# Operand halves moved from GpSimd to VectorE, and pooling and Fourier steps reordered, in an fp32 hybrid encoder layer

## Chip, cores and metric

One core of a Trainium2 chip runs the whole kernel. The metric is the device time of one execution in microseconds; the time given for a kernel is the median over its runs.

## What is computed

One encoder layer over two sequences, 4096 and 2048 tokens of 1024 channels, all in float32:

```python
h = rms_norm(x, pre_g)
proj = jnp.einsum('bsd,de->bse', h, w_in)
a_u, a_v, a_gate, b_in, b_gate, c_in, c_gate = jnp.split(proj, offsets, axis=-1)
ya = mixer_a(a_u, a_v, a_ln_g, a_ln_b, a_w_s, a_b_s) * jax.nn.silu(a_gate)  # gMLP, 128x128 mix per head
yb = mixer_b(b_in, b_w, b_scale) * jax.nn.silu(b_gate)   # centred means over 2, 4, 8, 16 tokens, minus identity
yc = mixer_c(c_in, c_w) * jax.nn.silu(c_gate)            # real part of a 2-D Fourier transform, per 64 channels
y = jnp.einsum('bse,ed->bsd', jnp.concatenate([ya, yb, yc], axis=-1), w_out)
return x + rms_norm(y, post_g)
```

## The kernel before

Every large matrix product is done in the seven-product form of fast matrix multiplication: operands and weights are cut into quadrants, summed, and multiplied seven times; the products are named P1, P2, X1, X2, Y1, X3 and Y2. Each factor is a float32 number in two parts: ScalarE rounds it to a high part (`split`, L137, a CAST in the trace) and a subtraction gives the low part (L138, TENSOR_TENSOR). TensorE then multiplies high by high, low by high and high by low (`mm3`, L141 to L143). The low part of an operand is 128x2048 and is made as two halves of 128x1024; before the change VectorE makes one half and GpSimd the other.

There are four passes. The first (0 to 490 us) goes over 12 blocks of 512 tokens: it normalises, makes the seven operands of a block (`operands`, four sums L177 to L191), stores them in DRAM and multiplies them for the Fourier branch. A scheduler orders its instructions. The second (490 to 959 us, operands b_P1 and so on) loads the operands again for the pooling branch, and the third (959 to 1437 us, a_P1 and so on) does so for the gMLP branch. The fourth, from 1437 us, is the output projection with its own operands.

The second and third pass are written by hand as slots, six blocks of 1024 tokens with seven slots each, one slot for each product. A slot loads the operand of two slots later, cuts the operand of the next slot (cast and low halves), and runs three products, one for each of three channel tiles (PSUM tiles Pb, Ab and Yb in the second pass, Pa, Ya and Aa in the third). Between them stand `fill_a` and `fill_b` (pooling, gating, normalising), the evictions of PSUM by `evict`, and `beside`, which runs one step of the Fourier branch. Four engines and the DMA queue of SyncE (SP) all execute in the order written. The slot of X1 adds to the PSUM banks that P1 has just filled, after the copy of P1's product (zb, L1318) has been made on ScalarE.

`beside` is called twice in a slot. A step has up to four parts: `load`, `pre`, `compute` and `store`. `steps` is a list: tables of the gMLP and channel mix (`table_steps`; their matmul prs reads ws), ten folds (`fold_steps`; VectorE subtractions L949 and L951, then a split), and the transforms (levels, `eg` and `T`; base steps; mix steps, whose matmuls pmx read the split th and tl, and at the end of each pair pny, which reads cny). `normalise` (L1408) issues 16 activations on ScalarE; it stands in `fill_a` of the third pass's slots P2 and X3.

Of the kernel before, what the change touches and what calls it, by code (L numbers as in the profile page):

```python
# [33 lines left out]
def hybrid_encoder(  # L34
# [722 lines left out]
    for b in range(NB):  # L757
        blk = nblk
        if b + 1 < NB:
            nxs = load_x(b + 1, xt, "p")  # L760
            nblk = Block(b + 1)
        for i, m in enumerate(ORDER):
            op = ready.pop(0)
            if b > 0 or i > 2:
                blk.product(m, op)
            if b == 0 and 0 < i < 4:
                rest_of_weights(i)
            if b > 0 or i > 1:
# [116 lines left out]
    def table_steps():  # L885
# [211 lines left out]
    def mix_steps(s, pair, kb):  # L1097
# [49 lines left out]
        if kb == S // 2 // TB - 1:  # L1147
            out[1] = Step(compute_ny, load_ny, None, store_ny)
# [63 lines left out]
    def pool_means(z, n, t, name, corr_at=None):  # L1212
# [7 lines left out]
        if t == 0:  # L1220
            V.tensor_add(b[96:, to], a[96:, 7 : n + 7], a[96:, 9 : n + 9])
            nc.scalar.copy(a[96:, to], b[96:, to])
        else:
            V.tensor_add(b[:, 2 : n + 15], a[:, 1 : n + 14], a[:, 3 : n + 16])
            if t == 1:
                V.tensor_add(a[64:, to], b[64:, 6 : n + 6], b[64:, 10 : n + 10])
                nc.scalar.copy(a[0:64, to], b[0:64, to])
            else:
                c = e1.tile([P, TB + 16], F32, tag="w", name=f"pc{name}", bufs=2)
                V.tensor_add(c[:, 4 : n + 13], b[:, 2 : n + 11], b[:, 6 : n + 15])  # L1230
                V.tensor_add(a[0:96, to], c[0:96, 4 : n + 4], c[0:96, 12 : n + 12])
                nc.scalar.copy(a[96:, to], c[96:, to])
# [4 lines left out]
        return a  # L1237

    class PoolBlock:


        def __init__(self, b):
# [59 lines left out]
        def close_sequence(self):  # L1302
# [30 lines left out]
    for b in range(NB // 2):  # L1333
        blk = PoolBlock(b)
        pairs = [Wide(t, f"b{b}_{t}") for t in range(3)]
        p = before
        means = lambda who, h, t: lambda: who.means(h, t)
        fa = {
            0: [lambda: blk.new_z(0)], 1: [lambda: blk.new_g(0)], 2: [],
            3: [lambda: blk.new_g(1), means(blk, 0, 0)], 4: [means(blk, 0, 2)],  # L1340
            5: [lambda: blk.new_z(1), lambda: blk.silu(1)], 6: [blk.keep_ends, means(blk, 1, 0)],
        }
        fb = {i: [] for i in range(7)}
        fb[3], fb[6] = [means(blk, 0, 1)], [means(blk, 1, 1)]
        if p:
            fa[0] += [lambda: p.silu(0), lambda: p.means(1, 2)]
            fb[0] += [lambda: p.gate(0)]
            fa[1] += [lambda: p.gate(1)]
            fa[2] += [p.close_sequence]
        for i, m in enumerate(WIDE["b"]):  # L1350
# [7 lines left out]
            slot(7 * b + i, pairs, lambda t, ps, m=m, blk=blk: blk.evict(m, t, ps), fa[i], fb[i], loads, None, cuts)  # L1358
        before = blk
# [194 lines left out]
    for b in range(NB // 2):  # L1554
# [38 lines left out]
        for i, m in enumerate(WIDE["a"]):  # L1593
            ev = lambda t, ps, m=m, blk=blk: blk.evict(m, t, ps)
            j = 7 * (b + NB // 2) + i
            if b == 0 and i == 0:
# [283 lines left out]
```

## Time and profile before

| | us |
|---|---|
| median of 3 runs | 1918.48 (1915.41 to 1920.11) |
| the profiled execution | 1926.82 |
| its span | 1925.0 |
| TensorE busy | 1762.3 (92% of the span) |
| VectorE busy | 1384.2 (72%) |
| ScalarE busy | 919.4 (48%) |
| GpSimd busy | 839.7 (44%) |

Busy time of an engine counts from start to end of each instruction, with whatever it waits inside. The granted TensorE clock was 0.96 of full speed on the mean.

### The profile page before, as it was taken

The numbers are of one execution on the slowest core, as the hardware profiler recorded it, in microseconds if no ns is written. First come the engines' busy times: TensorE is split into PE (matmuls) and PEld (weight loads), VectorE is DVE, ScalarE is ACT, GpSimd is POOL, SyncE is SP. The second block draws the span as 40 slices with busy tenths as digits, with TensorE's granted clock in tenths as the row PEclk, the third lists the DMA queues.
The fourth block names the chain that finished last, engine by engine and source line by source line (L and its number), as shares of the span: only waits on it lengthen the run. The fifth ranks groups of instructions, "written<-read, shape, count | busy, mean of one in ns | idle before, by whom it ended". The sixth has DMA issues, their size and how long they took to land. (4 is left out here: it accounts for less than half of the span.)

```text
span 1925.0 us, 27890 instructions
## 1 busy us (share of the span) xinstructions
PE 1762.3 (92%) x9784; PEld 1509.0 (78%) x9784; DVE 1384.2 (72%) x2163; ACT 919.4 (48%) x1766; POOL 839.7 (44%) x464
## 2 busy tenths in 40 slices
PE   5999999999878887988879999899988999999998
PEld 5999999999767666877668778787766888888876
DVE  8877767777588787667666575555677777877776
ACT  4766654444454443435445554555663433333332
POOL 6433664675332222222332332223355666666664
PEclk9999999999999998999889999999998999999999
DMA  6999997896669877757676675765644454545443
GB/s 243 316 335 313 368 343 271 290 325 234 224 217 307 263 253 252 260 202 236 232 258 228 234 256 188 246 206 195 198 156 159 159 169 158 170 159 169 158 160 109
DMA packets 221787, 443.84 MB, mean 231 GB/s; under 512 B 30416, under 2 KB 112976, under 8 KB 221648
## 3 DMA queue, kind: packets, MB, share of 16 engines
q1 hardware_dynamic: 221648, 442.07, 67.1%
q8 instruction: 77, 1.26, 0.3%
q14 instruction: 62, 0.51, 0.1%
HBM read 297.81 MB, written 150.47 MB: 233 GB/s over the span
## 5 line engine op out<-in xcount | busy, mean ns | idle before, releaser
L1712 POOL TENSOR_TENSOR cc<-cc,xr 128x1024 f32<-128x1024 f32 x46 | 110.3, 2398 | 53.5 <-DVE cc L1711 53.5
L1408 ACT ACTIVATE vn<-vn,lnst 128x96 f32<-128x96 f32 x192 | 70.2, 453 | 54.6 <-DVE lnst L1403 54.6
L398 DVE SCALAR_TENSOR_TENSOR xp<-xp,g_sb,rbc 128x256 f32<-128x256 f32 x192 | 92.5, 549 | 2.1 <-PE rbc L607 1.3
L1653 ACT ACTIVATE junk<-cc 128x512 f32<-128x512 f32 x72 | 45.5, 632 | 86.3 <-DVE cc L1694 51.8
L137 ACT CAST yo_X<-y 128x512 fp32r<-128x512 f32 x60 | 34.9, 620 | 87.9 <-PE Xo L143 71.9
L138 DVE TENSOR_TENSOR yo_P<-y,yo_P 128x512 fp32r<-128x512 f32 x48 | 69.5, 1449 | 6.4 <-ACT yo_P L137 6.1
L1711 DVE SCALAR_TENSOR_TENSOR cc<-cc,orr,pgb 128x512 f32<-128x512 f32 x69 | 53.8, 807 | 15.2 <-POOL orr L1661 15.2
L1218 DVE TENSOR_TENSOR pa<-zb 128x527 f32<-128x527 f32 x36 | 64.5, 1792 | 0.0
L1661 POOL TENSOR_TENSOR orr<-oms,mhalf 128x1 f32<-128x1 f32 x48 | 27.0, 562 | 84.5 <-DVE oms L1659 84.5
L177 POOL TENSOR_TENSOR s<-xp,xp 128x1024 f32<-128x1024 f32 x11 | 26.5, 2408 | 82.5 <-DVE xp L398 68.5
L138 DVE TENSOR_TENSOR yo_X<-y,yo_X 128x512 fp32r<-128x512 f32 x48 | 58.9, 1227 | 0.2
L365 ACT ACTIVATE xrow<-xrow 128x512 f32<-128x512 f32 x88 | 54.8, 627 | 7.3 <-DMA xrow<-in_x_sample 7.2
L141 PE MATMUL Ab<-b_X1h,wbX1h 128*128 128x512 f32 x72 | 32.6, 453 | 21.1 <-ACT zb L1318 21.1
L177 DVE TENSOR_TENSOR ys<-y,y 128x512 f32<-128x512 f32 x24 | 27.1, 1132 | 34.2 <-DMA y<-yc_d 33.8
L1653 ACT ACTIVATE junk<-Po 128x512 f32<-128x512 f32 x24 | 14.4, 599 | 74.7 <-PE Po L143 74.7
L1398 POOL TENSOR_TENSOR lnst<-lnst,mhalf 128x16 f32<-128x16 f32 x12 | 35.7, 2972 | 29.2 <-DVE lnst L1397 29.2
L137 ACT CAST yo_P<-y 128x512 fp32r<-128x512 f32 x48 | 29.4, 614 | 39.1 <-PE Xo L143 26.1
L191 POOL TENSOR_TENSOR y<-y,y 128x512 f32<-128x512 f32 x23 | 31.5, 1369 | 35.0 <-DVE yo_X L138 29.4
L1394 DVE BATCH_NORM_STATS2 lnst<-vn 128x6 f32<-128x96 f32 x192 | 44.1, 230 | 0.0
L138 POOL TENSOR_TENSOR a_X3l<-a_X3l,a_X3h 128x1024 fp32r<-128x1024 f32 x6 | 14.6, 2438 | 64.8 <-ACT a_X3h L137 64.8
L138 POOL TENSOR_TENSOR a_Y2l<-a_Y2l,a_Y2h 128x1024 fp32r<-128x1024 f32 x6 | 14.5, 2422 | 63.8 <-ACT a_Y2h L137 50.1
L377 DVE TENSOR_SCALAR diag<-ident,rr 128x128 f32<-128x128 f32 x44 | 40.9, 982 | 1.9 <-POOL rr L353 1.1
(778 smaller groups left out, 7122.7 us busy)
## 6 DMA issues: line engine op xcount, KB each, us to landing
op_d<-xp SPq DMA_DIRECT2D x72, 512.0 KB, 5.0
mt<-const_m SPq DMA_DIRECT2D x56, 512.0 KB, 6.4
xp<-in_xt SPq DMA_DIRECT2D x48, 512.0 KB, 5.5
out<-cc SPq DMA_DIRECT2D x46, 512.0 KB, 2.9
xr<-in_x_sample SPq DMA_DIRECT2D x32, 512.0 KB, 4.3
xrow<-in_x_sample SPq DMA_DIRECT2D x28, 512.0 KB, 5.7
o<-o_d SPq DMA_DIRECT2D x40, 256.0 KB, 5.7
vn_d<-vg SPq DMA_DIRECT2D x48, 192.0 KB, 3.6
```

The lines of the kernel that those rows point to most:

```text
L137: last_cast[0] = nc.scalar.copy(hi, src)
L138: return (nc.gpsimd if pool_lo else nc.vector).tensor_sub(lo, src, hi.bitcast(F32))
L177: e[0].tensor_add(s1, a21, a22)
L365: nc.scalar.activation(half, half, AF.Square, accum_out=ss[:, 2 * c + h : 2 * c + h + 1])
L377: nc.vector.tensor_scalar_mul(diag[:, c], ident, rr[:, 2 * a + c : 2 * a + c + 1])
L398: nc.vector.scalar_tensor_tensor(xs[q][:, sl], xs[q][:, sl], g8_sb[:, 4 * kh + k : 4 * kh + k + 1], rbc[a], ALU.mult, ALU.mult,)
L1218: V.tensor_add(a[:, 1 : n + 16], z[:, 0 : n + 15], z[:, 1 : n + 16])
L1394: nc.vector.bn_stats(st[:, j], self.v[h][c][:, 96 * hd : 96 * hd + 96])
L1408: nc.scalar.activation(v_, v_, AF.Identity, bias=nb[:, j : j + 1], scale=rv[:, j : j + 1])
L1653: nc.scalar.activation(junk, src, AF.Square, accum_out=ss[:, j : j + 1])
L1711: nc.vector.scalar_tensor_tensor(cc[c][:, hs], src, rr, pgb[:, hs], ALU.mult, ALU.mult)
L1712: nc.gpsimd.tensor_add(cc[c], cc[c], xr[c])
```

## The change

1. In the first pass all operand sums and the low parts of X2 and X3, which GpSimd made, go to VectorE; in the second and third pass VectorE makes both halves of each low part, and the low parts of the wide weights and of the output weights.
2. `pool_means` becomes a generator with a stop between its sums with the ScalarE copy and its last step on VectorE (`sums`, then `means` one place later); in a P1 slot the sums stand ahead of the three silu activations.
3. A step's `pre` runs two steps ahead of its `compute` instead of one, its `store` two behind instead of one; the four table steps move behind two folds and become six, and each base pair gets one empty step behind it.
4. In a second-pass slot the stores of yb go behind the first eviction, three at a time. The tiles of gny and cny get a ring of their own, and cny is made in a `pre`. One `next_y` is issued earlier at the start of the fourth pass.

```diff
-    SUMS0 = (nc.gpsimd, nc.vector, nc.gpsimd, nc.gpsimd)
+    SUMS0 = (nc.vector,) * 4
...
-    make = make_operand("p0", ("X2", "X3"))
+    make = make_operand("p0")
...
-                split(lo[:, h].bitcast(F32), hi[:, h], lo[:, h], h == 1)
+                split(lo[:, h].bitcast(F32), hi[:, h], lo[:, h])
...
-        for eng, sl in ((nc.vector, slice(0, 2)), (nc.gpsimd, slice(2, 3))):
-            eng.tensor_sub(lo[:, sl], lo[:, sl].bitcast(F32), hi[:, sl].bitcast(F32))
+        nc.vector.tensor_sub(lo, lo.bitcast(F32), hi.bitcast(F32))
...
-        if i <= len(steps):
-            part(i - 1, "store")
+        if i <= len(steps) + 1:
+            part(i - 2, "store")
             part(i + 2, "load")
             part(i, "compute")
-            part(i + 1, "pre")
+            part(i + 2, "pre")
...
-        return [Step(compute, load), Step(compute_mix, load_mix), Step(), Step()]
+        return [Step(), Step(), Step(compute, load), Step(compute_mix, load_mix), Step(), Step()]
...
-        return [Step(load), copies.pop(0), Step(compute), Step(store)]
+        return [Step(load), copies.pop(0), Step(compute, store=store), Step()]
...
         for which in range(2):
             out.append(base_step(s, pair, which))
+        out.append(Step())
...
+        def prepare_ny():
+            st["c"] = fpool.tile([P, 1], F32, tag="n", name=f"cny{nm}", bufs=4)
+            nc.scalar.activation(st["c"], T_of[(s, pair)][:, S // 2 : S // 2 + 1], AF.Copy, scale=scale)
+
         def compute_ny():
-            col_ = ftile(f"cny{nm}", (P, 1))
-            nc.scalar.activation(col_, T_of[(s, pair)][:, S // 2 : S // 2 + 1], AF.Copy, scale=scale)
...
-    steps[0:0] = table_steps()
+    steps[8:8] = table_steps()
...
-        flush(stores)
+        if not late:
+            flush(stores)
...
         evict(0, ps)
+        if late:
+            done, stores[:] = stores[:late], stores[late:]
+            flush(done)
         beside()
...
-            5: [lambda: blk.new_z(1), lambda: blk.silu(1)], 6: [blk.keep_ends, means(blk, 1, 0)],
+            5: [lambda: blk.new_z(1), lambda: blk.silu(1)], 6: [blk.keep_ends, sums(blk, 1, 0)],
         }
         fb = {i: [] for i in range(7)}
-        fb[3], fb[6] = [means(blk, 0, 1)], [means(blk, 1, 1)]
+        fb[3], fb[6] = ([sums(blk, h, 1), means(blk, h, 0)] for h in range(2))
+        fb[4] = [means(blk, 0, 2)]
         if p:
-            fa[0] += [lambda: p.silu(0), lambda: p.means(1, 2)]
-            fb[0] += [lambda: p.gate(0)]
+            fa[0] += [lambda: p.sums(1, 2), lambda: p.means(1, 1), lambda: p.silu(0)]
+            fb[0] += [lambda: p.means(1, 2), lambda: p.gate(0)]
...
-        split(lo[k].bitcast(F32), hi[k], lo[k], k % 2 == 1)
+        split(lo[k].bitcast(F32), hi[k], lo[k])
...
         cut_out_weights(m)
+        if m == "Y1":
+            next_y()
```

ScalarE at the P1 slot of the second pass's third block, before: the cast of the next operand (X1), the silu of the block before (gb), the last pooling copy (pa from pc), the copy of P1's first product (zb from Ab).

```order
L137 CAST b_X1h<-b_X1l 128x1024 x2
L1261 COPY zb_0_0_6757<-edge 128x16
L1261 COPY zb_0_1_6759<-edge 128x16
L1261 COPY zb_0_2_6761<-edge 128x16
L1274 ACTIVATE gb_0_0_6286<-gb_0_0_6286 128x512
L1276 COPY gb_1_0_6434<-gb_0_0_6286 128x8
L1274 ACTIVATE gb_0_1_6287<-gb_0_1_6287 128x512
L1276 COPY gb_1_1_6435<-gb_0_1_6287 128x8
L1274 ACTIVATE gb_0_2_6288<-gb_0_2_6288 128x512
L1276 COPY gb_1_2_6436<-gb_0_2_6288 128x8
L1232 COPY pa_1_2_6769<-pc_1_2_6773 32x512
L1318 COPY zb_0_0_6757<-Ab_0_6744 128x512
```

The same place on ScalarE in the changed kernel:

```order
L137 CAST b_X1h<-b_X1l 128x1024 x2
L1270 COPY zb_0_0_6728<-edge 128x16
L1270 COPY zb_0_1_6730<-edge 128x16
L1270 COPY zb_0_2_6732<-edge 128x16
L1239 COPY pa_1_2_6734<-pc_1_2_6738 32x512
L1283 ACTIVATE gb_0_0_6265<-gb_0_0_6265 128x512
L1285 COPY gb_1_0_6406<-gb_0_0_6265 128x8
L1283 ACTIVATE gb_0_1_6266<-gb_0_1_6266 128x512
L1285 COPY gb_1_1_6407<-gb_0_1_6266 128x8
L1283 ACTIVATE gb_0_2_6267<-gb_0_2_6267 128x512
L1285 COPY gb_1_2_6408<-gb_0_2_6267 128x8
L1331 COPY zb_0_0_6728<-Ab_0_6715 128x512
```

The pooling copy, which waits for VectorE, now stands ahead of the three silu activations, so these stand between it and the copy of P1's product.

VectorE at the same hand-over, before, from the low half of P1 to the low half of X1 (pa, pb: pooling sums; gb from Yb: eviction of Y2):

```order
L138 TENSOR_TENSOR b_P1l<-b_P1l,b_P1h 128x1024
L1218 TENSOR_TENSOR pa_1_0_6685<-zb_1_0_6595 128x527
L1221 TENSOR_TENSOR pb_1_0_6686<-pa_1_0_6685 32x512
L1236 SCALAR_TENSOR_TENSOR pa_1_0_6685<-pa_1_0_6685,cols,zb_1_0_6595 128x512
L1330 TENSOR_TENSOR gb_0_0_6286<-Yb_0_6513,gb_0_0_6286 128x512
L1218 TENSOR_TENSOR pa_1_1_6712<-zb_1_1_6597 128x527
L1224 TENSOR_TENSOR pb_1_1_6713<-pa_1_1_6712 128x525
L1226 TENSOR_TENSOR pa_1_1_6712<-pb_1_1_6713 64x512
L1236 SCALAR_TENSOR_TENSOR pa_1_1_6712<-pa_1_1_6712,cols,zb_1_1_6597 128x512
L1330 TENSOR_TENSOR gb_0_1_6287<-Yb_1_6544,gb_0_1_6287 128x512
L1330 TENSOR_TENSOR gb_0_2_6288<-Yb_2_6561,gb_0_2_6288 128x512
L138 TENSOR_TENSOR b_X1l<-b_X1l,b_X1h 128x1024
```

The end of the same stretch on VectorE in the changed kernel; the eight subtractions that begin this fold (L948) stand right ahead of these rows, and the two halves of P1 ahead of them:

```order
L950 TENSOR_TENSOR fz_2048_000_6590<-fz_2048_000_6590,fz_2048_004_6592 128x512
L138 TENSOR_TENSOR fo_2048_00_6656<-fo_2048_00_6656,fh_2048_00_6667 128x512
L950 TENSOR_TENSOR fz_2048_012_6594<-fz_2048_012_6594,fz_2048_016_6596 128x512
L138 TENSOR_TENSOR fo_2048_01_6657<-fo_2048_01_6657,fh_2048_01_6671 128x512
L1224 TENSOR_TENSOR pa_1_1_6686<-zb_1_1_6569 128x527
L1230 TENSOR_TENSOR pb_1_1_6687<-pa_1_1_6686 128x525
L1232 TENSOR_TENSOR pa_1_1_6686<-pb_1_1_6687 64x512
L1244 SCALAR_TENSOR_TENSOR pa_1_0_6650<-pa_1_0_6650,cols,zb_1_0_6567 128x512
L1343 TENSOR_TENSOR gb_0_1_6266<-Yb_1_6518,gb_0_1_6266 128x512
L1343 TENSOR_TENSOR gb_0_2_6267<-Yb_2_6533,gb_0_2_6267 128x512
L138 TENSOR_TENSOR b_X1l<-b_X1l,b_X1h 128x1024 x2
L1224 TENSOR_TENSOR pa_1_2_6734<-zb_1_2_6571 128x527
```

Both halves of P1 and X1 are here now, and the last step of each pooling tile (L1236, now L1244) has moved behind the sums of the next.

ScalarE in the P2 slot of the third pass's second block, before (vn: `normalise`):

```order
L137 CAST a_X2h<-a_X2l 128x1024 x2
L1408 ACTIVATE vn_0_9600<-vn_0_9600,lnst_0_9851 128x96 x4
L1408 ACTIVATE vn_1_9602<-vn_1_9602,lnst_0_9851 128x96 x4
L1408 ACTIVATE vn_2_9604<-vn_2_9604,lnst_0_9851 128x96 x4
L1408 ACTIVATE vn_3_9606<-vn_3_9606,lnst_0_9851 128x96 x4
L137 CAST a_X3h<-a_X3l 128x1024 x2
```

and in the changed kernel:

```order
L137 CAST a_X2h<-a_X2l 128x1024 x2
L1423 ACTIVATE vn_0_9567<-vn_0_9567,lnst_0_9822 128x96 x4
L1423 ACTIVATE vn_1_9569<-vn_1_9569,lnst_0_9822 128x96 x4
L1423 ACTIVATE vn_2_9571<-vn_2_9571,lnst_0_9822 128x96 x4
L1423 ACTIVATE vn_3_9573<-vn_3_9573,lnst_0_9822 128x96 x4
L1044 COPY ev_4096_1_9987<-pd_4096_10_9173 128x512
L1045 ACTIVATE eg_4096_1_9988<-pd_4096_10_9173,cols 128x512
L137 CAST a_X3h<-a_X3l 128x1024 x2
```

The work of a level (ev, eg), which stood in the slot before, has come to stand behind the sixteen activations; cny, which stood there in the third, fourth and fifth block, has left these slots.

## Rows read from the trace of the kernel before

**Rows 1.** Windows of the first two passes: length, busy us of each engine, clock, DMA.

```profile
core 0: us, PE busy (x) PEld busy (x) DVE busy (x) ACT busy (x) POOL busy (x), PEclk, DMA share, GB/s
0.00:490.00 490.00, 455.32 (x3202) 448.94 (x3203) 373.56 (x562) 266.15 (x519) 262.60 (x136) 0.98 0.86 303
490.00:959.00 469.00, 399.62 (x1650) 320.96 (x1649) 340.85 (x457) 209.36 (x372) 130.84 (x66) 0.92 0.73 244
```

**Rows 2.** TensorE's waits, 490 to 1437 us: total, times, longest.

```profile
PE Ab L141 <- ACT zb L1318: 21.1, 5, 8.7
PE pny L1140 <- ACT cny L1138: 17.4, 4, 4.5
...
PE pmx L141 <- ACT th L137: 8.8, 3, 4.2
PE prs L901 <- DMA ws<-in_ws_t: 7.2, 1, 7.2
PE pd L141 <- ACT eg L1045: 7.1, 4, 4.4
PE pd L141 <- DMA mt<-const_m: 6.7, 2, 4.6
PE Yb L142 <- DVE b_Y2l L138: 6.5, 2, 3.4
PE Ab L142 <- POOL b_X3l L138: 4.9, 3, 2.0
```

**Rows 3.** Windows of single slots and of pairs of slots, columns as in rows 1.

```profile
591.40:599.56 8.16, 8.16 (x38) 6.76 (x36) 2.98 (x4) 2.48 (x3) 2.43 (x1) 1.00 0.95 272
497.78:515.20 17.42, 10.22 (x46) 7.83 (x44) 7.01 (x11) 5.89 (x9) 3.74 (x5) 0.80 0.60 198
539.68:567.30 27.62, 19.78 (x74) 15.27 (x72) 24.06 (x38) 12.51 (x25) 9.65 (x4) 0.88 0.59 200
567.30:591.40 24.10, 19.26 (x74) 15.34 (x72) 23.69 (x35) 12.67 (x27) 5.85 (x2) 0.86 0.77 269
635.00:660.01 25.01, 19.16 (x74) 15.02 (x72) 22.46 (x35) 12.40 (x26) 8.03 (x3) 0.86 0.73 231
711.16:738.70 27.54, 18.82 (x74) 15.07 (x73) 26.37 (x44) 11.94 (x25) 5.85 (x2) 0.81 0.60 203
...
915.37:931.97 16.60, 12.88 (x44) 9.72 (x43) 12.09 (x14) 5.72 (x7) 4.75 (x2) 0.79 0.51 175
1143.41:1160.01 16.60, 12.31 (x45) 9.72 (x44) 6.13 (x7) 8.41 (x20) 2.43 (x1) 0.79 0.66 221
```

**Rows 4.** Timeline around the P1 slot at 635 us: start, us, engine, instruction.

```profile
632.95 2.90 DVE L1218 TENSOR_TENSOR pa<-zb 128x527 f32<-128x527 f32 x1
...
638.52 0.70 DVE L1218 TENSOR_TENSOR pa<-zb 128x527 f32<-128x527 f32 x1
...
643.79 2.86 DVE L1218 TENSOR_TENSOR pa<-zb 128x527 f32<-128x527 f32 x1
...
642.65 3.43 POOL L138 TENSOR_TENSOR b_X1l<-b_X1l,b_X1h 128x1024 fp32r<-128x1024 f32 x1 [7.37 <-ACT b_X1h L137]
...
642.74 0.63 ACT L1274 ACTIVATE gb<-gb 128x512 f32<-128x512 f32 x1
...
648.16 0.61 ACT L1232 COPY pa<-pc 32x512 f32<-32x512 f32 x1 [3.04 <-DVE pc L1230]
```

**Rows 5.** Window behind the wait that ended at 649.43, columns as in rows 1.

```profile
649.43:656.23 6.80, 6.80 (x20) 5.41 (x21) 6.77 (x17) 4.77 (x10) 0.54 (x1) 0.64 0.38 116
```

**Rows 6.** Groups of instructions: VectorE's half of operand X3, third pass.

```profile
L138 DVE TENSOR_TENSOR a_X3l<-a_X3l,a_X3h 128x1024 fp32r<-128x1024 f32 x6 | 7.4, 1226 | 7.6 <-ACT a_X3h L137 7.6
```

**Rows 7.** Groups of instructions: the activations of `normalise`.

```profile
L1408 ACT ACTIVATE vn<-vn,lnst 128x96 f32<-128x96 f32 x192 | 70.2, 453 | 54.6 <-DVE lnst L1403 54.6
```

**Rows 8.** Windows of a block late in the first pass, and around the fourth pass's start.

```profile
375.20:414.30 39.10, 36.13 (x258) 35.30 (x257) 30.02 (x45) 16.03 (x26) 26.91 (x14) 1.00 0.95 319
...
1424.00:1470.00 46.00, 32.82 (x110) 24.34 (x111) 38.10 (x44) 20.73 (x38) 20.45 (x13) 0.81 0.42 141
```

More of the change, by code (lines that the diff above doesn't have):

```diff
@@ L776, in hybrid_encoder @@
                     stream = operands(
-                        nxs, rpool.tile([P, 1024], F32, tag="s3", name=f"s3_{b + 1}"), make_operand(f"p{b + 1}", ("X2", "X3")),
+                        nxs, rpool.tile([P, 1024], F32, tag="s3", name=f"s3_{b + 1}"), make_operand(f"p{b + 1}"),
                         ORDER, SUMS0, normaliser(b + 1, nxs, nrbc), keep_operand(b + 1),
@@ L1132, in load_ny @@
         def load_ny():
-            st["g"] = ftile(f"gny{nm}", (P, 1))
+            st["g"] = fpool.tile([P, 1], F32, tag="n", name=f"gny{nm}", bufs=4)
             nc.sync.dma_start(st["g"], gc_d[s][rows, S // 2 : S // 2 + 1])
+        def prepare_ny():
+            st["c"] = fpool.tile([P, 1], F32, tag="n", name=f"cny{nm}", bufs=4)
+            nc.scalar.activation(st["c"], T_of[(s, pair)][:, S // 2 : S // 2 + 1], AF.Copy, scale=scale)
         def compute_ny():
-            col_ = ftile(f"cny{nm}", (P, 1))
-            nc.scalar.activation(col_, T_of[(s, pair)][:, S // 2 : S // 2 + 1], AF.Copy, scale=scale)
             ps = wide_bank("G", f"pny{nm}")
-            nc.tensor.matmul(ps[:, 0:1], cmix[pair][0], col_, start=True, stop=True)
+            nc.tensor.matmul(ps[:, 0:1], cmix[pair][0], st["c"], start=True, stop=True)
             nc.vector.tensor_mul(st["g"], st["g"], ps[:, 0:1])
@@ L1147, in mix_steps @@
         if kb == S // 2 // TB - 1:
-            out[1] = Step(compute_ny, load_ny, None, store_ny)
+            out[1] = Step(compute_ny, load_ny, prepare_ny, store_ny)
         return out
@@ L1166, in flush, with slot @@
             f()
-    def slot(j, pairs, evict, fill_a=(), fill_b=(), loads=(), then=None, cuts=()):
+    def slot(j, pairs, evict, fill_a=(), fill_b=(), loads=(), then=None, cuts=(), late=False):
         m = todo[j][2]
         load_operand(j + 2)
-        flush(stores)
+        if not late:
+            flush(stores)
         for f in loads:
@@ L1221, in pool_means @@
             V.tensor_add(b[96:, to], a[96:, 7 : n + 7], a[96:, 9 : n + 9])
-            nc.scalar.copy(a[96:, to], b[96:, to])
+            rows, src = slice(96, P), b
         else:
@@ L1226, in pool_means @@
                 V.tensor_add(a[64:, to], b[64:, 6 : n + 6], b[64:, 10 : n + 10])
-                nc.scalar.copy(a[0:64, to], b[0:64, to])
+                rows, src = slice(0, 64), b
             else:
@@ L1231, in pool_means @@
                 V.tensor_add(a[0:96, to], c[0:96, 4 : n + 4], c[0:96, 12 : n + 12])
-                nc.scalar.copy(a[96:, to], c[96:, to])
+                rows, src = slice(96, P), c
+        nc.scalar.copy(a[rows, to], src[rows, to])
+        yield a
         if corr_at is not None:
@@ L1236, in pool_means @@
         V.scalar_tensor_tensor(a[:, to], a[:, to], invw[t], z[:, to], ALU.mult, ALU.subtract)
-        return a
+        yield a
     class PoolBlock:
@@ L1247, in __init__ @@
             self.pooled = [[None] * 3 for _ in range(2)]
+            self.half = {}
         def new(self, lst, h, tag, extra, bufs):
@@ L1278, in silu, with sums, means @@
                     nc.scalar.copy(ends[t][:, 16:24], self.g[1][t][:, TB : TB + 8])
-        def means(self, h, t):
-            self.pooled[h][t] = pool_means(
+        def sums(self, h, t):
+            self.half[h, t] = pool_means(
                 self.z[h][t], TB, t, f"{self.b}_{h}_{t}", (16, 0) if self.t0 == 0 and h == 0 else None
             )
+            next(self.half[h, t])
+        def means(self, h, t):
+            self.pooled[h][t] = next(self.half[h, t])
         def keep_ends(self):
@@ L1308, in close_sequence @@
                 nc.gpsimd.tensor_copy(zl[t][:, 0:16], ends[t][:, 0:16])
-                a = pool_means(zl[t], 8, t, f"{self.b}_{t}l", (8, 8))
+                *_, a = pool_means(zl[t], 8, t, f"{self.b}_{t}l", (8, 8))
                 nc.vector.tensor_mul(a[:, 8:16], a[:, 8:16], ends[t][:, 16:24])
@@ L1337, in hybrid_encoder @@
         means = lambda who, h, t: lambda: who.means(h, t)
+        sums = lambda who, h, t: lambda: who.sums(h, t)
         fa = {
             0: [lambda: blk.new_z(0)], 1: [lambda: blk.new_g(0)], 2: [],
-            3: [lambda: blk.new_g(1), means(blk, 0, 0)], 4: [means(blk, 0, 2)],
-            5: [lambda: blk.new_z(1), lambda: blk.silu(1)], 6: [blk.keep_ends, means(blk, 1, 0)],
+            3: [lambda: blk.new_g(1), sums(blk, 0, 0)], 4: [sums(blk, 0, 2), means(blk, 0, 1)],
+            5: [lambda: blk.new_z(1), lambda: blk.silu(1)], 6: [blk.keep_ends, sums(blk, 1, 0)],
         }
         fb = {i: [] for i in range(7)}
-        fb[3], fb[6] = [means(blk, 0, 1)], [means(blk, 1, 1)]
+        fb[3], fb[6] = ([sums(blk, h, 1), means(blk, h, 0)] for h in range(2))
+        fb[4] = [means(blk, 0, 2)]
         if p:
-            fa[0] += [lambda: p.silu(0), lambda: p.means(1, 2)]
-            fb[0] += [lambda: p.gate(0)]
+            fa[0] += [lambda: p.sums(1, 2), lambda: p.means(1, 1), lambda: p.silu(0)]
+            fb[0] += [lambda: p.means(1, 2), lambda: p.gate(0)]
             fa[1] += [lambda: p.gate(1)]
@@ L1357, in hybrid_encoder @@
                     cuts.append(lambda i=i: cut_wide_weights(WIDE["b"][i - 2]))
-            slot(7 * b + i, pairs, lambda t, ps, m=m, blk=blk: blk.evict(m, t, ps), fa[i], fb[i], loads, None, cuts)
+            slot(7 * b + i, pairs, lambda t, ps, m=m, blk=blk: blk.evict(m, t, ps), fa[i], fb[i], loads, None, cuts, 3)
         before = blk
@@ L1604, in hybrid_encoder @@
                     f()
+                prev.means(1, 1)
+                prev.sums(1, 2)
                 prev.silu(0)
@@ L1628, in hybrid_encoder @@
     cut_out_weights("X2")
-    assert at[0] > len(steps)
+    assert at[0] > len(steps) + 1
     by_hand.close()
```

## Prediction

> **What bounds it now.** I began with the windows of the passes [rows 1]. TensorE is busy for 455.3 of 490.0 us in the first pass and 399.6 of 469.0 in the second, where its mean clock is 0.92. The second pass is where time is lost, so I read what TensorE waits for there and in the third pass, and then the slots of those waits.
>
> A slot that waits for nothing takes 8.16 us for its 36 matmuls, 0.227 each [rows 3]. With a step of six matmuls that makes 9.52, with seven 9.75. (The counts in the rows hold one or two neighbours at the edges.) What a slot takes beyond this is its loss. The list of waits names seven things in front of TensorE [rows 2]: copies of P1's product (zb 21.1), cny 17.4, th 8.8, the load of ws 7.2, eg 7.1, the load of mt 6.7, and late low halves (b_Y2l 6.5, b_X3l 4.9).
>
> Each long wait costs more than itself. The wait that ended at 649.43 is followed by 6.80 us with 20 matmuls at a granted clock of 0.64 [rows 5]; at full pace they take 20 x 0.227 = 4.5, so 2.3 us go to the lower of the two clock levels (1.2 instead of 2.4 GHz) behind the idle time. [...]
>
> The timeline of the P1 slot shows why VectorE is late there [rows 4]: the same 128x527 addition takes 0.70 us alone, and 2.86 when it starts at 643.79 while GpSimd makes its half of b_X1l (642.65, 3.43 us). It ends at 646.65, 0.57 after GpSimd's, as if it had begun only then. The one at 632.95 takes 2.90. GpSimd's half thus costs VectorE about 2.2 us each time, and it is not free for having been given away.
>
> The Trainium skill ("SBUF — State Buffer", Who interferes with whom) says that VectorE and GpSimd share a port pair as an exclusive lock, the loser being fully blocked; the trace agrees: the 0.70 addition took 2.86.
>
> **What a moved half costs and gives.** On VectorE a half of 128x1024 takes 1.23 us [rows 6]; on GpSimd 2.43 (its one instruction in the free slot [rows 3]). So an operand needs 2.4 of VectorE in a row where it needed 1.2 beside 2.4 of GpSimd: it is ready no later, and the 2.2 that an overlapped addition lost come back. An operand whose GpSimd half was hidden costs VectorE 1.2 that TensorE doesn't see as long as VectorE has idle time: 340.9 busy of 469 in the second pass [rows 1], 2.98 of 8.16 in the free slot [rows 3].
>
> *Late halves, second pass.* Before: 6.5 + 4.9 = 11.4 in five waits, and some four times 2.3, 20.6 in all. I keep one case: the X3 and Y2 slots of the first block lose 27.62 - 16.32 = 11.3 with VectorE busy 24.1 of 27.6 [rows 3], and there VectorE, not GpSimd, is late; I leave 8 of it. **-13** (ends 0 and -20.6).
>
> *Hand-over P1 to X1.* X1 waits for the copy of P1's product, which stands on ScalarE behind the last pooling copy; that copy sat idle 3.04 us for VectorE's pc [rows 4]. The three pairs in rows 3 lose 24.10, 25.01 and 27.54 less 16.32: 7.8, 8.7, 11.2, sum 27.7; without 2.3 for the clock the waits are 5.5, 6.4, 8.9. In the changed order VectorE saves two stretched additions (-4.4) and makes X1's second half (+1.2); the three silu with their small copies, 0.83 each or 2.5 (0.63 and the rest to the next, [rows 4]), now stand behind the pooling copy and ahead of the copy of P1 (+2.5). A fold of twelve VectorE instructions (17 in 6.77 us [rows 5], so about 4.8) still stands ahead of the X1 half in the third block, and no longer in the second and fourth (-4.8 each). This gives 0, 5.7 and 3.4; with the clock, and 1 for the first, 1 + 8.0 + 5.7 = 14.7. **-13** (ends 0 and -27.7).
>
> *First pass.* Five instructions a block go over, 5 x 1.23 = 6.1 us on VectorE, which is busy 30.0 of 39.1 in one of the densest blocks, part of it stretched by GpSimd's 26.9 [rows 8]. 36.1 in all, as much as TensorE's 36.1 there; about half of GpSimd's time is gone, and its stretching with it. TensorE hides the added work while VectorE stays below that. The 3 us that TensorE idles in such a block should shrink in a few blocks. **-4** (ends -9 and +12, if each of 12 blocks runs 1 us over).
>
> *Start of the fourth pass.* TensorE idles 46.0 - 32.8 = 13.2 us with VectorE busy 38.1 [rows 8]. Output weights cut by VectorE alone don't wait for GpSimd, but add to its queue. **-5** (ends 0 and -13).
>
> **Steps.** *Table.* The second pass begins with a slot of 17.42 us whose table matmul waits 7.2 for ws [rows 2, 3]. It moves behind two folds: 17.42 - 9.52 = **-7.9**, hidden by eight more `beside` calls between.
>
> *th and cny.* Slots where th is made one call ahead take 16.60, a loss of 7.1 [rows 3]; of the three waits (8.8 us) two are long: 14.2. The third pass's P2 slots wait for cny behind the 16 activations of `normalise`, 0.45 us each and overlapping [rows 7], ScalarE being busy 8.41 in the slot: 16.60 - 9.75 = 6.8 [rows 3], three times, and one shorter wait of 4.5 in the second pass. Sum **-39.2**. But the order shows that six inserted calls move other steps into that place: ev and eg stand behind the 16 activations in the third pass's second block, base steps and T copies in its fourth and fifth. Three slots lose again, at the price of the same place, 6.8 each and 1.5 more for ev and eg: **+22** (ends 0 and +26).
>
> *eg and mt.* Waits of 7.1 and 6.7, the longest 4.4 and 4.6 [rows 2]; their steps fall elsewhere by six calls. I take half off: **-3** and **-4** (ends +7 and -18 together).
>
> *Stores and loads on SP.* Fold stores go one slot later and operand loads stop queueing behind them; the fold's own loads come behind `evict(0)` with them, a product and a half later (some 4 us). A late fold load blocks VectorE and all the pooling behind it. **+4** (ends 0 and +30).
>
> Sum: -13 -13 -4 -5 -7.9 -39.2 +22 -3 -4 +4 = -63. The profiled execution took 1926.8, so 1863.7; the median before is 8.3 lower, so **1855 us**.
>
> **Rivals.**
> *A, the hand-overs and P2 slots close too.* Without GpSimd's lock VectorE runs ahead, and the steps in P2 slots find their inputs ready: 14.7 + 22 more, 1855 - 37 = **1818**. For it: 2.98 of 8.16 in the free slot. Against it: the order on ScalarE, which the lock doesn't touch.
>
> *B, moving work off GpSimd is worth nothing in the slots.* VectorE is busy in 24.1 of 27.6 or 22.5 of 25.0 us just where it is late [rows 3]; the added 1.2 per operand takes what the lock gave. Then late halves, hand-overs and the fourth pass's start stay: 13 + 13 + 5, so **1886**. The order part alone pays.
>
> The Trainium skill ("Perfetto Trace Analysis", Optimizing Scalar/DVE Operations) says that offloading between GpSimd and VectorE might not help since they share a port, and that a saturated VectorE may be relieved by GpSimd. By the first half the change gives B, by the second even a loss; the trace, with 0.70 against 2.86, speaks for taking the work back.
>
> *C, the other side: VectorE becomes the bound of the first pass.* If its idle time there (39.1 - 30.0 = 9.1 a block) is dependence on other engines and cannot shrink, each of 12 blocks grows by 6.1, or 73: 1855 + 73 = **1928**. It decides where VectorE's work with its waits passes TensorE's 36.1 a block. Against it: half of GpSimd's time leaves the block.
>
> **Numbers.** Forecast 0.52 (1855, its own range 1836 to 1872), A 0.20, B 0.18, C 0.06, and 0.04 that part of C and B cancel the gain to within 0.3%, about what a measurement of this kernel can tell from no change. Faster 0.90, same 0.04, slower 0.06. The range reaches just past A and B, 1812 to 1890.
>
> **What would show it.** The 128x527 additions stay at 0.70 and no VectorE instruction with two SBUF operands is stretched in the second and third pass; the waits for ws, cny, th and b_X3l are gone; a wait in P2 slots names eg, bm or T; hand-overs lose about 15; block lengths of the first pass stay near 36 to 39. I am wrong if the first pass grows beyond some 495 us, if SP's fold loads hold up VectorE, or if the losses in the slots return under a VectorE name.

## The result and the profile after

The changed kernel takes 1873.92 us (1871.57 to 1875.73 in four runs) against 1918.38 (1915.41 to 1920.11 in four): ratio 0.9769, 95% interval 0.9752 to 0.9787. The forecast was 1855, with 1812 to 1890 as its range. The profiled execution took 1875.17 us with a span of 1873.4.

The windows of the four passes, columns as in [rows 1]:

```profile
0.00:483.73 483.73, 453.34 (x3201) 447.49 (x3201) 385.47 (x622) 264.44 (x519) 100.62 (x76) 0.99 0.86 307
483.73:894.21 410.48, 379.77 (x1640) 308.76 (x1639) 315.29 (x487) 207.09 (x370) 3.90 (x18) 0.96 0.81 272
894.21:1388.97 494.76, 445.88 (x2932) 365.44 (x2930) 316.94 (x752) 262.71 (x479) 37.27 (x12) 0.94 0.63 215
1388.97:1873.40 484.43, 466.08 (x2017) 379.71 (x2015) 365.78 (x460) 182.41 (x400) 287.57 (x187) 0.98 0.48 160
```

The second pass is 58.7 us shorter (469.2 to 410.5), the first 5.9, the fourth 3.8 (488.2 to 484.4; the passes are cut at their first matmul here, in [rows 1] at round numbers). The third is 16.7 us longer (478.0 to 494.8). VectorE took over 42 halves in the second pass (some ten of its other instructions left the pass) and is busy less long than before, 315.3 us against 340.9: its own instructions are no longer stretched. In the list of instruction groups the 128x527 addition, whose mean was 1.79 us before, has this row:

```profile
L1224 DVE TENSOR_TENSOR pa<-zb 128x527 f32<-128x527 f32 x36 | 25.2, 701 | 0.1
```

The Trainium skill ("Perfetto Trace Analysis", Optimizing Scalar/DVE Operations) says that offloading between GpSimd and VectorE might not help; here taking the offloaded work back helped (the engine moves alone gave a ratio of 0.9801, below).

TensorE's waits in the second and third pass, as in [rows 2]:

```profile
PE Ab L141 <- ACT zb L1331: 13.7, 3, 6.0
PE pny L1142 <- ACT ua L1474: 13.1, 1, 13.1
PE pd L141 <- ACT eg L1045: 9.9, 4, 5.6
PE pd L141 <- DMA mt<-const_m: 6.7, 3, 4.0
PE pbs L1088 <- ACT T L1060: 4.6, 1, 4.6
...
PE pbc L1088 <- ACT bm L1090: 3.9, 1, 3.9
PE Yb L142 <- DVE b_Y2l L138: 3.7, 1, 3.7
```

The waits for ws, cny and the long ones for th are gone, and so are those for GpSimd, which made 9.8 us together before (4.9 of them in [rows 2]). Four others have grown: ua at the start of the third pass (9.2 before, on another matmul), T (0.8), bm (1.9) and eg (7.1). Single slots and pairs, those of [rows 3] first, then the start of the third pass and its P2 slots:

```profile
491.89:500.05 8.16, 8.16 (x38) 6.76 (x36) 2.44 (x2) 4.27 (x5) 0.00 (x0) 1.00 0.96 356
525.69:552.62 26.93, 19.90 (x81) 15.11 (x82) 24.76 (x43) 12.97 (x26) 0.00 (x0) 0.87 0.50 161
552.62:573.43 20.81, 18.00 (x73) 14.49 (x72) 14.62 (x24) 10.94 (x26) 0.00 (x0) 0.92 0.68 225
614.36:638.34 23.98, 17.96 (x73) 14.44 (x72) 22.13 (x38) 12.58 (x27) 0.00 (x0) 0.86 0.88 301
680.60:704.95 24.35, 19.43 (x74) 15.49 (x72) 22.95 (x38) 12.51 (x26) 0.00 (x0) 0.86 0.62 203
721.27:738.02 16.75, 12.71 (x43) 9.60 (x42) 12.24 (x17) 5.30 (x8) 0.00 (x0) 0.80 0.80 278
863.99:873.59 9.60, 9.60 (x43) 7.88 (x42) 8.34 (x10) 3.48 (x5) 0.00 (x0) 1.00 0.68 246
894.21:936.20 41.99, 24.41 (x87) 19.25 (x86) 31.39 (x79) 13.86 (x24) 2.90 (x1) 0.76 0.68 229
1009.97:1028.25 18.28, 11.93 (x44) 9.38 (x43) 5.79 (x9) 9.38 (x21) 0.00 (x0) 0.81 0.40 144
1091.54:1101.52 9.98, 9.82 (x43) 7.81 (x42) 7.24 (x17) 6.84 (x16) 2.90 (x1) 1.00 0.61 213
1170.70:1186.51 15.81, 11.88 (x53) 9.91 (x52) 5.15 (x8) 10.20 (x23) 1.41 (x1) 0.89 0.35 112
1254.01:1270.41 16.40, 11.77 (x46) 9.61 (x44) 4.20 (x6) 8.99 (x22) 0.00 (x0) 0.79 0.28 89
```

The table's slot is free (8.16 from 17.42), the second th slot nearly (9.60 from 16.60). The pair at 894.21, P1 and X1 of the third pass's first block, took 34.63 before and takes 41.99 now. The P2 slots of the third, fourth and fifth block took 16.6 each and take 9.98, 15.81 and 16.40; that of the second went from 9.64 to 18.28.

ScalarE in this last slot, from the timeline (start, us, engine, instruction, idle time before), and TensorE's matmul that waited for it:

```profile
1010.66 2.00 ACT L137 CAST a_X2h<-a_X2l 128x1024 fp32r<-128x1024 f32 x2
1014.23 5.84 ACT L1423 ACTIVATE vn<-vn,lnst 128x96 f32<-128x96 f32 x16 [1.57 <-DVE lnst L1418]
1019.97 0.56 ACT L1044 COPY ev<-pd 128x512 f32<-128x512 f32 x1
1020.44 0.68 ACT L1045 ACTIVATE eg<-pd,cols 128x512 f32<-128x512 f32 x1
...
1021.17 0.58 PE L141 MATMUL pd<-mt,o 128*128 128x256 f32 x1 [5.59 <-ACT eg L1045]
```

The sixteen activations begin 1.57 us late, since the small VectorE instruction that they need stands behind both halves of X2; then ev and eg stand behind them for 5.84 us.

### The profile page after: what moved, and what is told of

Same layout as the page of the kernel before. It is cut to its first block, busy times and chain, and to the rows that moved or that the text cites. A ratio compares the mean times of both kernels' runs of the same rounds, so it can differ in the third digit from the quotient of the medians.

```text
span 1873.4 us, 27630 instructions
## 1 busy us (share of the span) xinstructions
PE 1745.1 (93%) x9784; PEld 1501.4 (80%) x9784; DVE 1383.5 (74%) x2320; ACT 916.6 (49%) x1766; POOL 429.4 (23%) x293
## 5 line engine op out<-in xcount | busy, mean ns | idle before, releaser
L398 DVE SCALAR_TENSOR_TENSOR xp<-xp,g_sb,rbc 128x256 f32<-128x256 f32 x192 | 98.8, 580 | 4.7 <-ACT rbc L382 3.2
L353 POOL TENSOR_TENSOR rr<-ssq,mhalf 128x4 f32<-128x4 f32 (+1 forms) x13 | 17.0, 1311 | 201.7 <-DVE ssq L351 138.9
L141 PE MATMUL pd<-mt,o 128*128 128x256 f32 (+1 forms) x80 | 27.9, 349 | 24.1 <-ACT eg L1045 9.9
L137 ACT CAST yo_P<-y 128x512 fp32r<-128x512 f32 x48 | 29.4, 615 | 40.1 <-PE Xo L143 26.1
L1239 ACT COPY pa<-pb 32x512 f32<-32x512 f32 (+1 forms) x24 | 14.8, 619 | 58.6 <-DVE pb L1227 36.5
L1410 DVE BATCH_NORM_AGGREGATE lnst<-lnst 128x2 f32<-128x6 f32 x192 | 35.0, 182 | 6.6
```

The costliest lines, as they stand in the source:

```text
L137: last_cast[0] = nc.scalar.copy(hi, src)
L141: nc.tensor.matmul(ps, lh, rh, start=first, stop=False, skip_group_check=True)
L398: nc.vector.scalar_tensor_tensor(xs[q][:, sl], xs[q][:, sl], g8_sb[:, 4 * kh + k : 4 * kh + k + 1], rbc[a], ALU.mult, ALU.mult,)
```

## The experiments

All ratios are to the kernel before, on the same chip. Differences in us to the changed kernel are between medians of different chips, on which the kernel before took 1918.4 to 1920.9 us.

**Engines alone, order alone, first pass alone, and one mend.** Engines alone:

```diff
-    SUMS0 = (nc.gpsimd, nc.vector, nc.gpsimd, nc.gpsimd)
+    SUMS0 = (nc.vector,) * 4
...
-    make = make_operand("p0", ("X2", "X3"))
+    make = make_operand("p0")
...
-                split(lo[:, h].bitcast(F32), hi[:, h], lo[:, h], h == 1)
+                split(lo[:, h].bitcast(F32), hi[:, h], lo[:, h])
...
-            eng.tensor_sub(lo[:, sl], lo[:, sl].bitcast(F32), hi[:, sl].bitcast(F32))
+        nc.vector.tensor_sub(lo, lo.bitcast(F32), hi.bitcast(F32))
...
-        split(lo[k].bitcast(F32), hi[k], lo[k], k % 2 == 1)
+        split(lo[k].bitcast(F32), hi[k], lo[k])
```

> The kernel before with the engine moves alone (sums, low halves and weight parts on VectorE in the first three passes), everything in the old order. My theory, GpSimd's instructions hold up VectorE: late halves -13, three hand-overs from P1 to X1 some -12 (two stretched additions off, one half more, and the clock once), first pass -4, start of the fourth pass -5, so about 1884 against 1918; the 128x527 additions all take 0.70. Rival, VectorE is full at these places and the added halves take what is gained: 1912 to 1920, the gain of the whole change then comes from the order.

Measured: 1884.56, ratio 0.9801 (0.9774 to 0.9827). The additions take 0.701 on the mean. Its second and third pass:

```profile
481.22:924.84 443.62, 395.24 (x1652) 318.91 (x1651) 323.39 (x497) 209.81 (x372) 3.90 (x18) 0.93 0.77 259
924.84:1394.02 469.18, 437.98 (x2920) 358.46 (x2919) 309.97 (x742) 261.61 (x476) 36.45 (x12) 0.96 0.64 220
```

25.6 and 8.8 us shorter. The rival, a full VectorE, falls. The gain, 36 us between the medians, is what the theory had, but not where the theory had it, so its size is partly luck. The three hand-overs from P1 to X1 lost 25.2 instead of 27.7 us, 2.5 less where 12 were expected (the waits for zb went from 4.8, 5.9 and 8.7 to 5.0, 3.6 and 8.6), and the slots of the late halves gave 9.5 of 13. About as much again came from slots with a step, whose waits for ws, mt, eg, th and cny grew shorter, and from the third pass, for which the theory had no term.

Order alone: the same lines taken back in the changed kernel, as

```diff
-                split(lo[:, h].bitcast(F32), hi[:, h], lo[:, h])
+                split(lo[:, h].bitcast(F32), hi[:, h], lo[:, h], h == 1)
```

> The changed kernel with the engine moves undone (GpSimd makes its halves, sums and weight parts again), the new order kept. My theory: table -8, th and cny -39 with 22 given back in the third pass's P2 slots, eg and mt -7, loads +4, so about 1890; the additions are stretched again to a mean near 1.8. Rival, the order carries the change: 1874 to 1878.

Measured: 1911.86, ratio 0.9951 (0.9935 to 0.9967), and additions of 2.13 us on the mean. Neither guess holds. The passes show why:

```profile
486.07:921.95 435.88, 384.88 (x1640) 310.79 (x1639) 336.71 (x446) 205.53 (x370) 130.18 (x65) 0.95 0.76 256
921.95:1419.70 497.75, 440.83 (x2932) 361.17 (x2930) 312.00 (x708) 263.44 (x478) 158.86 (x69) 0.95 0.63 214
```

In the second pass the new order gives 33.3 us, in the third it takes 19.7 back. The two parts add in the medians: 0.9801 x 0.9951 = 0.9753 against 0.9769. In the windows 25.6 + 33.3 = 58.9 us of the second pass meet 58.7 in the whole change, but that is partly chance: the execution profiled here took 1902.14 us, 9.7 below its median, that of the engines alone 5.8 below and that of the kernel before 8.3 above, so the windows overstate both parts, and slot by slot they do not add (the hand-overs gave 2.5 and 1.8 us alone and 7.5 together).

The first pass alone:

```diff
-    SUMS0 = (nc.gpsimd, nc.vector, nc.gpsimd, nc.gpsimd)
+    SUMS0 = (nc.vector,) * 4
...
-    make = make_operand("p0", ("X2", "X3"))
+    make = make_operand("p0")
```

> The kernel before with the first pass's sums and low halves on VectorE, nothing else. My theory: TensorE hides the added 6.1 us of VectorE a block, and its idle time shrinks a little: the first pass 2 to 6 us shorter, 1912 to 1916 in all. Rival, VectorE becomes the bound of some blocks: the first pass 5 us or more longer.

Measured: 1918.15, ratio 0.9985 (0.9971 to 0.9998), 2.8 us between the medians; the first pass took 485.9 against 489.6. My theory holds, if barely. Single profiles of kernels with this same first pass gave 481.2 to 486.4, and the order-alone kernel, whose first pass is the old one, gave 486.1; so the windows do not separate the two, and the gain rests on the medians.

The mend of the P2 slots:

```diff
...
+        def shift(self, h):
             st, mv, va, rv, nb = self.ln[h]
             nc.vector.scalar_tensor_tensor(nb, mv[:, :, 0], -1.0, rv, ALU.mult, ALU.mult)
-            for c in range(NCH):
+
+        def normalise(self, h, cs=range(NCH)):
...
-        fa[2].append(lambda: blk.normalise(0))
+        fa[2].append(lambda: blk.normalise(0, range(2)))
+        fb[2].append(lambda: blk.normalise(0, range(2, 4)))
...
+        fb[1].append(lambda: blk.shift(0))
```

> The changed kernel with the sixteen activations of the third pass's P2 slot issued eight ahead of the first and eight ahead of the second call of beside, and the small VectorE instruction they need issued a slot earlier. My theory, steps wait in P2 slots only for their place in ScalarE's order: the three long P2 slots (18.3, 15.8, 16.4) come to 10 to 12, in all -12 to -18, so about 1859 against 1874. Rival, these steps' own chain of matmul, copy and VectorE is late there wherever the activations stand: within 3 us of 1874.

Measured: 1845.43, ratio 0.9599 (0.9573 to 0.9625), 28.5 us below the changed kernel, more than the 12 to 18 expected. Its third pass and the three P2 slots that were long:

```profile
896.98:1362.34 465.36, 433.18 (x2932) 356.11 (x2931) 317.75 (x752) 261.97 (x479) 37.28 (x12) 0.97 0.67 229
1011.22:1022.83 11.61, 9.40 (x43) 7.45 (x42) 5.89 (x9) 9.29 (x21) 0.35 (x1) 1.00 0.65 229
1162.13:1172.10 9.97, 9.97 (x53) 8.54 (x52) 4.75 (x7) 9.20 (x22) 1.56 (x1) 1.00 0.52 169
1237.30:1246.76 9.46, 9.35 (x46) 7.72 (x45) 4.16 (x6) 8.90 (x22) 0.09 (x1) 1.00 0.48 155
```

18.3 + 15.8 + 16.4 = 50.5 became 31.0, 19.4 of the 29.4 us by which the third pass is shorter; the clock is 1.00 in all three. The other 10 are spread over its neighbours, 1 to 3 us each, and were not traced one by one. ScalarE in the slot of the third pass's fourth block, in the changed kernel and here:

```profile
1171.43 2.00 ACT L137 CAST a_X2h<-a_X2l 128x1024 fp32r<-128x1024 f32 x2
1174.99 5.84 ACT L1423 ACTIVATE vn<-vn,lnst 128x96 f32<-128x96 f32 x16 [1.56 <-DVE lnst L1418]
1180.74 0.34 ACT L1090 ACTIVATE bm<-pbc,cols 128x128 f32<-128x128 f32 x1
...
1162.86 2.00 ACT L137 CAST a_X2h<-a_X2l 128x1024 fp32r<-128x1024 f32 x2
1164.76 2.98 ACT L1428 ACTIVATE vn<-vn,lnst 128x96 f32<-128x96 f32 x8
1167.63 0.35 ACT L1090 ACTIVATE bm<-pbc,cols 128x128 f32<-128x128 f32 x1
```

The step's bm came 9.31 us after the start of the cast and comes after 4.77. Of the 4.5 us, 1.7 are the earlier start of the activations (the VectorE instruction that was moved) and 2.9 their smaller number ahead of it. The place in ScalarE's order was the cause; the edit changes both things at once, so their shares of the 28.5 us are not separated.

**The hand-over, and GpSimd's hold on VectorE by itself.** Silu ahead of the pooling sums:

```diff
-            fa[0] += [lambda: p.sums(1, 2), lambda: p.means(1, 1), lambda: p.silu(0)]
+            fa[0] += [lambda: p.silu(0), lambda: p.sums(1, 2), lambda: p.means(1, 1)]
```

> The changed kernel with the three silu activations of a P1 slot back ahead of the pooling sums, the rest as changed. My theory, the silu stand 2.5 us between the last pooling copy and the copy of P1's product: the three hand-overs (together 68.9 us for six slots, 20 more than free slots) lose 2.5 each, and some of the clock with it, so 1862 to 1868 against 1874. Rival, ScalarE then waits in the silu for VectorE's eviction of Y2, and the pooling copy comes as late as before: within 3 us of 1874.

Measured: 1864.39, ratio 0.9717 (0.9691 to 0.9742), 9.5 below the changed kernel. The three pairs of P1 and X1:

```profile
549.76:567.32 17.56, 16.64 (x74) 13.44 (x72) 14.90 (x25) 10.95 (x26) 0.00 (x0) 1.00 0.62 203
608.22:630.06 21.84, 18.25 (x74) 14.58 (x72) 21.62 (x37) 12.38 (x27) 0.00 (x0) 0.92 0.99 323
672.28:693.66 21.38, 18.30 (x74) 14.40 (x72) 20.39 (x35) 12.51 (x26) 0.00 (x0) 0.92 0.54 192
```

They took 20.81, 23.98 and 24.35 in the changed kernel, so 3.3, 2.1 and 3.0 less: this part of the new order was a loss.

GpSimd work without use, first reading SBUF (h1 is 128x384 of the high part, scr a bf16 tile):

```diff
+    scr = e1.tile([P, 384], mybir.dt.bfloat16, name="scr")
+    nc.vector.memset(scr, 0.0)
...
+            h1 = hi[:, 1].bitcast(F32).rearrange("p k t -> p (k t)")[:, 0:384]
+            if n == "b":
+                for _ in range(3):
+                    nc.gpsimd.tensor_sub(scr, h1, h1)
             cut[j] = hi, lo
```

> The changed kernel with three GpSimd subtractions of 128x384 added behind each cast of the second pass, whose results nobody reads. Nothing waits for them but GpSimd's own order. My theory, a GpSimd instruction that reads SBUF holds up VectorE's instructions with two SBUF operands: the 128x527 additions go from 0.70 to above 1.0 on the mean, the second pass from 410 to 416 or more, 1880 to 1895 in all. Rival, GpSimd's halves cost time before only because TensorE waited for their results: 0.70 and 1874.

then writing only (scr is set up as above):

```diff
+            if n == "b":
+                nc.scalar.copy(scr[:, 0:1], hi[:, 1, 0, 0:1].bitcast(F32))
+                for _ in range(3):
+                    nc.gpsimd.memset(scr, 0.0)
```

> As the run before, but the three added GpSimd instructions are memsets that read nothing (a ScalarE copy of one column ties each to its cast). If what holds VectorE up is GpSimd reading SBUF, the additions stay at 0.70 and the time within 4 us of 1874. Rival, any GpSimd instruction on SBUF does it: the additions are stretched as in the run before.

Measured: 1914.16 (ratio 0.9972, 0.9955 to 0.999) with the subtractions, 1874.31 (0.9771, 0.9745 to 0.9796) with the memsets. The mechanism came as expected with the subtractions, the size did not: 40 us instead of 6 to 21. The second pass with the subtractions, its 128x527 additions, and the added instructions on one of the seven operands:

```profile
485.54:940.75 455.21, 392.35 (x1641) 316.07 (x1639) 382.76 (x495) 206.56 (x370) 175.98 (x150) 0.93 0.73 245
...
L1231 DVE TENSOR_TENSOR pa<-zb 128x527 f32<-128x527 f32 x36 | 38.4, 1066 | 0.1
...
L845 POOL TENSOR_TENSOR scr<-b_X2h 128x384 bf16<-128x384 f32 x18 | 22.5, 1251 | 32.5 <-ACT b_X2h L137 31.6
```

and with the memsets:

```profile
481.66:898.08 416.42, 380.87 (x1640) 309.00 (x1639) 323.38 (x494) 218.45 (x415) 55.70 (x150) 0.96 0.80 268
...
L1231 DVE TENSOR_TENSOR pa<-zb 128x527 f32<-128x527 f32 x36 | 25.2, 701 | 0.1
...
L845 POOL MEMSET scr<- 128x384 bf16 x126 | 52.7, 418 | 398.2 <-ACT scr L843 393.3
```

Work whose results nobody reads, and for which no cast waited, cost 40 us, nearly the whole gain. From the run with memsets to that with subtractions VectorE's busy time in the second pass goes from 323.4 to 382.8 with one instruction more, and the pass from 416.4 to 455.2. The memsets stretch no addition and cost nothing in the whole kernel; their second pass is 6 us longer than the changed kernel's 410.5 because its first slot takes 15.2 us instead of 8.2 (16.3 with the subtractions): VectorE sets up scr there in both runs and makes the first halves behind that. This shows the cause of the engine part: for the most part not late results of GpSimd, for which TensorE waited 9.8 us in all before, but its reading while VectorE wants two SBUF operands. The Trainium skill ("SBUF — State Buffer", SBUF: two separate sides) says that a VectorE instruction with two SBUF inputs takes the shared ports only against a GpSimd instruction that reads SBUF; the two runs agree, 1.07 against 0.70.

Later cuts of weights (besides X3 and Y1, that of Y2 moves, from the second slot to the fourth):

```diff
-                if i > 1:
+                if 1 < i < 6:
                     cuts.append(lambda i=i: cut_wide_weights(WIDE["b"][i - 2]))
...
-            ct[0].append(lambda: cut_wide_weights("X3"))
+            ct[1].append(lambda: cut_wide_weights("X3"))
             ld[0].append(lambda: load_wide_weights("a", "Y2"))
-            ct[1].append(lambda: cut_wide_weights("Y2"))
+            ct[2].append(lambda: cut_wide_weights("Y1"))
+            ct[3].append(lambda: cut_wide_weights("Y2"))
```

> The changed kernel with the cuts of two third-pass weights (Y1, X3) moved from the last slot of the second and the first of the third pass to the second and third slot of the third, where VectorE has idle time. My theory, the hand-over between the passes (42 us for two slots, some 23 more than they need) is set by VectorE's queue, which the waits of the old order had given time to empty: two cuts of 1.76 less ahead of it, 3 to 6 us shorter, about 1869. Rival, it is set by ScalarE's copies and the small end-of-sequence instructions behind them: within 2 us of 1874.

Measured: 1865.06, ratio 0.9723 (0.9699 to 0.9747), 8.9 below the changed kernel where 3 to 6 were expected. The pair at the start of the third pass:

```profile
892.37:930.09 37.72, 23.77 (x87) 18.80 (x86) 27.60 (x77) 12.19 (x22) 2.90 (x1) 0.77 0.74 254
```

41.99 became 37.72, with VectorE busy 27.6 instead of 31.4, nearly all of it in the P1 slot (23.2 to 19.1), which VectorE's queue sets; the X1 slot kept 18.6. Later slots of the third pass gave 3.6 more; the rest is spread over the other passes and lies within their scatter.

**Together.** The three mends in one kernel:

> The changed kernel with the three mends together: eight and eight activations in the P2 slots, silu ahead of the pooling sums, two weight cuts in the third pass's second and third slot. They act in different slots, so if each is what I take it for they add: 28.5 + 9.5 + 8.9 less, about 1827. Rival, the slots lean on the same VectorE and ScalarE queues and a wait closed in one returns in the next: 1836 or more.

and with the transforms two steps later:

```diff
-    steps.extend([Step(), Step()])
+    steps.extend([Step(), Step(), Step(), Step()])
```

> As the run before, with two more empty steps between the last fold and the first transform. In the changed kernel the transform's first matmul waits 4.0 us for mt, whose load stands on SP behind the eight stores of the last fold; one slot more lets it land: the slot of 16.75 comes to 9.5, -7 against the run before. Rival, the load is late for its landing, not its place in the queue, or the moved steps hit worse places in the third pass: within 3 us of the run before, or slower.

Measured: 1837.97 (0.9584, 0.9563 to 0.9605) and 1834.91 (0.9567, 0.9548 to 0.9586). The mends do not quite add: 36 us of 47, as the rival said. The first and the last mend both closed waits of the third pass, and the pair of its first block still took 38.1 us; that this overlap is the whole shortfall was not shown. The extra steps gave 3, within the two intervals, and not the 7 expected: with the mends alone the first matmul with mt already waits only 0.6 us, and the slot of Y1, 14.9 us there, keeps 12.6 with no step in it, waiting for VectorE's half of Y1. The last kernel is the fastest of all, 4.3% below the kernel before.

## Why the prediction was right, and where it was off

Direction and range held; the forecast gain of 63 us was 44.5. Seven of the 19 lie in the base: the profiled execution before was 8.3 us above its median, that of after 1.3 above its own, so the 63 stands against 51.6 between the two profiles. The terms, each against the slots:

- *Late halves*, -13: five slots behind the first block lost 11.3 less together, and the X3 and Y2 slots of the first block kept 10.6 of their 11.3 (8 was left). The number was right, the cause only in part: in the five slots the engines alone gave 5.4 and the order alone 7.5, most of it in the Y2 slot of the third block (13.79 to 8.16). The price of 2.3 us for the clock, read behind one wait, was added to four; it varies: the slot with the wait of 4.56 us for mt lost 3.1 beyond it, the one with a wait of 2.01 for b_X3l 0.4.
- *Hand-overs P1 to X1*, -13: 27.7 became 20.2, so -7.5. The 2.5 us for the silu behind the pooling copy were real (the run with silu first gave 8.4 in these pairs), but the first pair fell to 4.5, not to 1, and the last to 8.0, not to 5.7. That shorter additions would bring the copy of P1 forward showed in the third block alone (5.9 to 3.6 with the engines alone); alone, the engines gave 2.5 and the order 1.8.
- *Table*, -7.9: -9.3. *th and cny in the second pass*, -18.7: -19.5. *eg and mt*, -7: two slots gave 17.6, the transform's first matmul now waits 4.0 for mt behind the last fold's stores in SP's queue and another slot is 1.9 longer, 8.5 in all. *Loads*, +4: VectorE's waits for fold loads in the second pass, which the term was about, went from 3.1 to 4.0; a late load shows instead as that wait for mt, which is in the 8.5.
- *First pass*, -4: -2.8 between the medians of the run of the first pass alone; single windows, -3 to -8, scatter too much to say more. *Start of the fourth pass*, -5: -4.
- *P2 slots*, -20.5 and +22: the three that the order named lost 21.5 (8.8, 5.8 and 6.9 over a free slot of as many steps), so the net of the four P2 slots, +1.1 against +1.5, was right for the reason given: the waits there name eg, bm and T, as the prediction said they would, and the mend shows it.

The step that failed is one that wasn't there: the list of terms had none for the hand-over from the second to the third pass. TensorE's wait there stood third in the list of waits before, of which [rows 2] shows a part, and the prediction does not name it:

```profile
PE Aa L141 <- ACT ua L1459: 9.2, 1, 9.2
```

The hand-over lost 7.4 more, 10.3 with the new order alone (34.6 to 44.9), and gained 3.0 with the engines alone (31.65). ScalarE's ua stands behind VectorE's last pooling instruction. From the pass's first matmul to the end of that instruction, before and after:

```profile
958.78:976.94 18.16, 9.68 (x43) 7.69 (x41) 15.33 (x32) 6.78 (x13) 6.76 (x8) 0.86 0.56 189
...
894.21:916.29 22.08, 9.74 (x43) 7.69 (x41) 20.50 (x41) 7.76 (x16) 0.00 (x0) 0.81 0.47 157
```

VectorE has 41 instructions left there instead of 32, and TensorE waits 13.1 us. The likely reason is that the waits for th and cny in the last block of the second pass, some 20 us, had let VectorE finish more of the pooling before TensorE arrived; the later cuts, which took work out of this queue and shortened it, fit this, but no run gave the waits back alone. What I booked as -18.7 was then in part moved, not removed. The remaining 8 us of the third pass's loss are spread over slots into which other steps had moved; the mend of the P2 slots took about as much away, but which of them it reached is not separated.

Of the rivals, B fell with the run of the engines alone, -36 between the medians, though at the hand-overs from P1 to X1, where that run gave 2.5, it came nearer than the forecast. That the order would carry the change fell as well; it gave 9. A fell since the hand-overs kept 20.2 and the P2 slots lost 21.5, and C since the first pass did not grow.

## What to carry to other kernels

Work handed to GpSimd is not free for VectorE: count each GpSimd instruction that reads SBUF as time taken from VectorE's instructions with two SBUF operands (0.70 us became 2.9 beside a half), and compare a stretched row with a free one of the same shape before offloading. When waits of TensorE are removed just ahead of a place where it needs another engine's last instruction, ask how long that engine's queue still is; the wait may only move. In code with a fixed order, look at what stands behind a long run of small activations on ScalarE: splitting it in two, with its input made earlier, gave 28.5 us here, where the whole change gave 44.5.

## What the runs showed of the hardware that was not expected

GpSimd's memset of 128x384 (0.42 us, 126 of them) left VectorE's additions at 0.701 on the mean, the 17 of 36 that ran beside a memset included, while subtractions of the same size took them to 1.07: the 21 that ran beside one took 1.32 or 1.33, the other 15 stayed at 0.70. The hold goes both ways: the four added subtractions that met no VectorE instruction took 0.83 us, all of them 1.24 to 1.65 on the mean, by operand.

In the kernel before, what counts is which begins first. The 20 additions that began after a GpSimd subtraction ended 0.56 or 0.57 us after its end, whatever its length; the five that began first took 0.70, and the GpSimd half beside them took 2.56 to 2.88 us against 2.43 in the free slot. The 11 that met none took 0.70.
